# A hybrid attention and S5 block on one core: w_out split through PSUM, a second buffer for the GLU's inputs, other figures for the scheduler

## The chip, the core and the metric

The kernel runs on one core of a Trainium2 chip. Its engines are TensorE (PE, with its weight loads shown apart as PEld), VectorE (DVE), ScalarE (ACT) and GpSimd (POOL); SyncE (SP) issues nearly all DMAs. The time is device microseconds of one execution. Each engine works through its own queue in order, and an instruction that waits holds up all that stand behind it on that engine.

## What is computed

The layer normalises its input, projects it once, and feeds two groups of heads: latent attention, and an S5 state-space layer with a GELU and a GLU behind it. Each branch is gated and normalised, and both go through one output projection. Sequence 2048 + 16 meta tokens, width 1024, 8 heads (64 + 32 wide keys, 64 wide values), 32 groups of 16 channels.

```python
q = einsum('blr,re->ble', rmsnorm(q_lat, q_norm_w), w_q_up)      # + rotary part
kv = einsum('blr,re->ble', rmsnorm(kv_lat, kv_norm_w), w_kv_up)  # k_nope, v
y_attn = block_attention(qf, kf, vf)                             # softmax(q k / sqrt(96)) v
y_attn = rmsnorm(y_attn * silu(attn_gate), attn_out_norm_w)
y_ssm = gelu(s5(u, forward) + s5(u, backward) + ssm_d * u)
glu = einsum('ble,ef->blf', y_ssm, w_glu) + b_glu
y_ssm = rmsnorm(glu[..., :512] * sigmoid(glu[..., 512:]) * silu(ssm_gate), ssm_out_norm_w)
y = einsum('ble,ed->bld', concatenate([y_attn, y_ssm], -1), w_out)
return h + rmsnorm(y, post_norm_w)
```

All products of weights are made in three passes: each operand is split into a rounded high half and the low rest (`split`: ACT writes the high half, DVE subtracts it from the source for the low half), and high x high, high x low and low x high are summed in PSUM.

## The kernel before

Stages. First come projections and up-projections; then the gates' products (`pg`) run beside the S5 scan (`ssm_*`), whose last products are `py`. Behind the last `py`, `b_open` opens the pools of attention and issues the loads for it. Attention (`b_main`, `b_pv`) goes through 16 units, one for four query blocks of a pair of heads. A unit has 17 key tiles t and two heads h; for each, three products into a bank `sc`, an exponential by ACT into a buffer `pp`, an add by POOL into `acc[h]` (for the softmax's sums) and, in five groups, the products with V (`pv`). Beside unit u, `b_prep_q` makes unit u + 1's queries and their row maxima: 40 products `pm`, each followed by a `reduce_max` of DVE into `mx`; `b_kbuild` makes keys (`pk`), and `b_gate` prepares the gate `gt`. `finish` sums `acc` over partitions on PE (`sm`), takes reciprocals on DVE, sends them through DRAM (`rs_d`) to spread them over partitions (`sms`), multiplies `ot` twice on POOL and stores it to `ya_d`.

Also beside attention runs `glu_main`: it splits `w_glu` (`rawl` into `wl`), and for each of 8 blocks loads `ysv` (the S5 output) and `gv` (the gate), does GELU on DVE and ACT (`tg_c`, `ge_c`), 96 products `pa_c`, and stores `ysv` to `ys_d`. Then it loads `w_out` in eight slices (`rawo`), splits each (`wo`, the last low half is called `wo_l`) and scales the post-norm row `pw` on POOL. Only then does it start `c_stat` and `c_split`, the first steps of the output stage: `c_stat` loads a tile `yt`, squares it (`sq_c`), sums over partitions on PE (`pss`), and sends the sums through DRAM (`vvc`) to get the norm `rrc`; `c_split` splits `yt` into `yy`. `c_late` has the output products `po`, which `rrc` scales on their way out of PSUM, and `c_post` the post-norm.

What sets the order. The streams are Python generators. `Order.run` always continues the one whose inputs, banks and engine are free first by a cost model (`Clock`), and by rank among those that are free; a stream with a `due` above the current progress (in units of attention) goes after the others. `clock.lat` is what the model adds to each DMA. PE, ACT, DVE and POOL take their instructions in the order in which the streams were continued. PSUM banks go round in small rings: `pm` (banks 2, 3 and 6) is shared by row maxima, `tg`, `sm` and `pk`; the GLU has one bank. `PPB` is the number of `pp` buffers.

## Time and profile before

| | us |
|---|---|
| three timed runs | 1719.89, 1722.88, 1726.23 |
| median | 1722.88 |
| the profiled execution | 1720.63 |
| its span, first to last instruction | 1718.8 |
| PE busy in the span | 1654.9 (96%) |
| DVE, POOL, ACT busy | 1111.9 (65%), 819.4 (48%), 771.0 (45%) |
| mean granted clock of PE | 0.982 |

In the rows, L190 is a helper through which every instruction passes, so instructions are told apart by their tiles. A row of the timeline has the start and the length in us, the engine, the instruction with its output and inputs, their shapes, how many in a row were merged, and, in brackets, how long the engine stood before it and what ended that. PE's share says little by itself: what counts is where PE stands, and at what clock it goes on after that.

### The profile page before, as it was taken

The numbers are of one execution on the slowest core, as the hardware profiler recorded it, in microseconds if no ns is written. First come the engines' busy times: TensorE is split into PE (matmuls) and PEld (weight loads), VectorE is DVE, ScalarE is ACT, GpSimd is POOL, SyncE is SP. The second block draws the span as 40 slices with busy tenths as digits, with TensorE's granted clock in tenths as the row PEclk, the third lists the DMA queues.
The fourth block names the chain that finished last, engine by engine and source line by source line (L and its number), as shares of the span: only waits on it lengthen the run. The fifth ranks groups of instructions, "written<-read, shape, count | busy, mean of one in ns | idle before, by whom it ended". The sixth has DMA issues, their size and how long they took to land.

```text
span 1718.8 us, 28550 instructions
## 1 busy us (share of the span) xinstructions
PE 1654.9 (96%) x10320; PEld 1287.8 (75%) x10320; DVE 1111.9 (65%) x2531; ACT 771.0 (45%) x1604; POOL 819.4 (48%) x690
## 2 busy tenths in 40 slices
PE   7999999999999999999999999999998989989998
PEld 7897999999899866767757666776665655557776
DVE  5788635899994657555555647556555676476665
ACT  4543334445453255445444544445354534534442
POOL 0011012000000177776767688687788877862222
PEclk9999999999999999999999999999999999999999
DMA  8865735554354642012112110202012111124332
GB/s 214 269 202 142 224 125 169 145 174 145 102 164 129 171 117 82 22 54 75 38 53 72 50 58 29 90 26 70 29 40 71 41 56 43 38 99 141 119 114 86
DMA packets 179539, 175.68 MB, mean 102 GB/s; under 512 B 35419, under 2 KB 153110, under 8 KB 178118
## 3 DMA queue, kind: packets, MB, share of 16 engines
q1 hardware_dynamic: 179382, 173.86, 33.2%
q8 instruction: 81, 1.33, 0.3%
q14 instruction: 60, 0.49, 0.1%
q10 hardware_dynamic: 16, 0.00, 0.0%
HBM read 110.28 MB, written 63.54 MB: 101 GB/s over the span
## 4 chain that ended last, share of the span: by engine, by line
PE 69%; DVE 16%; DMA 6%; issue 4%; ACT 2%; SPq 1%; POOL 0%; DVEq 0%; ACTq 0%; POOLq 0%
PE sc L190 21%; PE po L190 9%; PE pm L190 8%; PE pa_c L190 5%; PE pg L190 4%; PE pu L190 3%; PE pa L190 3%; DVE w L190 2%; DVE wo L190 1%; DVE mct L190 1%; DVE s0t L190 1%; DVE r L190 1%; DMA sms<-rs_d 1%; PE pq L190 1%; DVE xx L190 1%
## 5 line engine op out<-in xcount | busy, mean ns | idle before, releaser
L190 POOL TENSOR_TENSOR acc<-acc,pp 128x512 f32<-128x512 f32 (+1 forms) x480 | 606.3, 1294 | 97.3 <-ACT pp L190 95.6
L190 ACT ACTIVATE pp<-sc 128x512 f32<-128x512 f32 (+1 forms) x544 | 320.3, 597 | 342.2 <-PE sc L190 308.7
L190 DVE TENSOR_REDUCE mx<-pm 128x1 f32<-128x412 f32 (+1 forms) x640 | 339.7, 578 | 144.5 <-PE pm L190 142.0
L190 PE MATMUL sc<-qh,kh 97*128 97x512 f32 (+1 forms) x544 | 224.4, 413 | 2.4 <-DVE qh L190 2.4
L190 PE MATMUL sc<-qh,kl 96*128 96x512 f32 (+1 forms) x544 | 220.7, 406 | 0.0
L190 PE MATMUL sc<-ql,kh 96*128 96x512 f32 (+1 forms) x544 | 218.5, 402 | 0.0
L190 PE MATMUL pm<-kh,qh 96*128 96x412 f32 (+1 forms) x640 | 196.1, 369 | 20.1 <-DVE mx L190 17.5
L190 PE MATMUL po<-wo,yy 128*128 128x512 f32 (+1 forms) x759 | 180.8, 391 | 0.0
L190 PEld LDWEIGHTS pm<-kh,qh 96*128 96x128 f32 x640 | 119.1, 194 | 78.9 <-DVE mx L190 27.6
L190 PEld LDWEIGHTS po<-wo,yy 128*128 128x128 f32 x759 | 139.7, 189 | 35.2 <-issue 3.0
L190 PE MATMUL pg<-x2h,wg_h 128*128 128x256 f32 x448 | 131.2, 293 | 3.8 <-ACT gs L190 3.8
L190 PEld LDWEIGHTS sc<-qh,kh 97*128 97x128 f32 (+1 forms) x544 | 102.3, 188 | 38.1 <-issue 19.2
L190 PE MATMUL pg<-x2h,wg_l 128*128 128x256 f32 x448 | 127.9, 286 | 0.0
L190 PE MATMUL pg<-x2l,wg_h 128*128 128x256 f32 x448 | 127.8, 285 | 0.0
L190 PEld LDWEIGHTS sc<-ql,kh 96*128 96x128 f32 (+1 forms) x544 | 103.1, 189 | 28.1
L190 POOL TENSOR_TENSOR ta<-qs,cs 128x512 f32<-128x512 f32 x8 | 10.9, 1363 | 222.0 <-ACT qs L190 148.4
L190 PEld LDWEIGHTS sc<-qh,kl 96*128 96x128 f32 (+1 forms) x544 | 103.3, 190 | 11.0
L190 POOL TENSOR_TENSOR t_c<-o_c,pw 128x512 f32<-128x512 f32 (+1 forms) x33 | 44.9, 1362 | 135.1 <-DVE o_c L190 118.9
L190 POOL COPY U<-um 128x4 f32<-128x4 f32 x16 | 4.8, 309 | 209.1 <-issue 145.2
L190 PE MATMUL pa_c<-gh,wl 128*128 128x256 f32 x512 | 103.8, 284 | 0.0
L190 PEld LDWEIGHTS pg<-x2h,wg_h 128*128 128x128 f32 x448 | 87.0, 194 | 4.8 <-ACT gs L190 4.4
L190 PEld LDWEIGHTS pa_c<-gh,wl 128*128 128x128 f32 x512 | 84.0, 190 | 6.7 <-issue 2.4
(456 smaller groups left out, 3364.7 us busy)
## 6 DMA issues: line engine op xcount, KB each, us to landing
raw<-in_x_dram SPq DMA_DIRECT2D x16, 512.0 KB
gate_d<-gs SPq DMA_DIRECT2D x64, 128.0 KB
md<-g_d SPq DMA_DIRECT2D x64, 128.0 KB
xt_c<-in_x_dram SPq DMA_DIRECT2D x8, 1024.0 KB
out_dram<-o_c SPq DMA_DIRECT2D x15, 512.0 KB
xt_d<-x3h SPq DMA_DIRECT2D x14, 512.0 KB
xt_d<-x3l SPq DMA_DIRECT2D x14, 512.0 KB
x2h<-xt_d SPq DMA_DIRECT2D x14, 512.0 KB
```

What stands on the lines that cost most here:

```text
L190: r = f(*args, **kw)
```

## The change

- `w_out`: each slice is now split in two halves of 512 columns. ACT writes the scaled half into a PSUM bank of the ring `pm` (`ws_o`), ACT copies it to the high half, and DVE subtracts with `ws_o` from PSUM as an input. Before, ACT scaled the whole slice into the high half, and DVE did scale and subtraction in one instruction with all inputs in SBUF. The due times go from 12.1 + 0.35 k to 12.6 + 0.36 k (+ 0.18 for the second half).
- `rawl` and `ysv`, which share a tag, have two buffers instead of one; the blocks' due times are 1.42 units apart instead of 1.3, and the products within a block are packed into 1.2 instead of 1.3.
- `clock.lat` is 4.0 instead of 2.0 from `b_open` on, and 2.2 instead of 0.95 after each unit.
- In unit 15 the sums of the last two key tiles go to DVE instead of POOL (four adds).
- `PPB` is 12 instead of 13, and `ones` has 32 columns instead of 64.
- In `ssm_x` the scheduler may turn to other streams between the four groups of scaled copies.

```diff
@@ -299,7 +299,7 @@
     cp = Pool(clock, "cp", ctx.enter_context(tc.tile_pool(name="cp", bufs=1, side="left")), 0.0)
     ident = cp.tile([P, P], F32, name="ident")
     make_identity(nc, ident)
-    ones = cp.tile([P, 64], F32, name="ones")
+    ones = cp.tile([P, 32], F32, name="ones")
     POOL.memset(ones, 1.0)
     cols = cp.tile([P, 27], F32, name="cols")
     half = cp.tile([P, 1], F32, name="half")
@@ -1387,6 +1387,7 @@
                 A.copy(xx[64:128, ri, 1, :, ::-1], xq[64:128])
 
             for o, x_, k in ((w1, xr, 0), (w2, xr, 1), (vr, vi, 2), (xr, vi, 0)):
+                yield Need(eng="A")
                 for q in range(NB):
                     c = slice(q * P, (q + 1) * P)
                     A.activation(o[:, c], x_[:, c], AF.Copy, scale=l8[:, k, b * NB + q:b * NB + q + 1])
@@ -1440,7 +1441,7 @@
     kh, kl, vps, qts = {}, {}, {}, {}
 
     def b_open():
-        clock.lat = 2.0
+        clock.lat = 4.0
         kp = open_pool("kp", "left")
         qp = open_pool("qp", "left")
         kw = open_pool("kw", "left")
@@ -1570,7 +1571,7 @@
             done[f"q{u}"] = 1
 
     FR = -1.5
-    PPB = 13
+    PPB = 12
     pps, accs = {}, {}
 
     gts = {}
@@ -1647,13 +1648,13 @@
                     if t == 1:
                         POOL.tensor_tensor(acc[h], first[h], pp, ALU.add)
                     elif t > 1:
-                        POOL.tensor_tensor(acc[h][:n], acc[h][:n], pp[:n], ALU.add)
+                        (V if u == 15 and t >= NJ - 1 else POOL).tensor_tensor(acc[h][:n], acc[h][:n], pp[:n], ALU.add)
                     if t == 0:
                         first.append(pp)
                     pps.setdefault((u, t), []).append(pp)
                     order.progress = u + (t + 0.5 * h + 0.5) / 17
             done["unit"] = u + 1
-            clock.lat = 0.95
+            clock.lat = 2.2
 
     def b_pv():
 
@@ -1687,7 +1688,7 @@
         NT = 256
         wl = gl.tile([P, 2, 4, D], F32R, name="wl")
         for k in range(4):
-            raw = gl.tile([P, D], F32, tag="ysv", name="rawl", bufs=1)
+            raw = gl.tile([P, D], F32, tag="ysv", name="rawl", bufs=2)
             SP.dma_start(raw, w_glu[k * P:(k + 1) * P, :].rearrange("(g h) f -> h g f", h=16))
             yield Need(raw, when=lambda: order.progress > 0.05)
             for hv in range(2):
@@ -1698,7 +1699,7 @@
                 split(wl[:, 0, k, c], wl[:, 1, k, c], ws)
         for b in range(8):
             bs = slice(b * NT, (b + 1) * NT)
-            ysv = gl.tile([P, 4, NT], F32, tag="ysv", name="ysv", bufs=1)
+            ysv = gl.tile([P, 4, NT], F32, tag="ysv", name="ysv", bufs=2)
             for t in range(2):
                 SP.dma_start(ysv[:, :, t * P:(t + 1) * P],
                              yr_d[:, 2 * b + t].rearrange("m h (g c) -> (h g) m c", c=P))
@@ -1706,7 +1707,7 @@
             SP.dma_start(gv, gate_d[4:8, :, bs].rearrange("m p c -> p m c"))
             gh = gl.tile([P, 4, NT], F32R, tag="gh", name="gh", bufs=1)
             gl_ = gl.tile([P, 4, NT], F32R, tag="sq", name="gl_", bufs=1)
-            d0 = 0.5 + b * 1.3
+            d0 = 0.5 + b * 1.42
 
             for hv in range(2):
                 h_ = slice(2 * hv, 2 * hv + 2)
@@ -1733,7 +1734,7 @@
                     for k in range(4):
                         if k % 2 == 0:
                             yield Need(gl_, banks=["gl"] if (half_, k) == (0, 0) else [],
-                                       due=d0 + (mm_ + 1) * 1.3 / 18)
+                                       due=d0 + (mm_ + 1) * 1.2 / 18)
                             mm_ += 1
                             if (half_, k) == (0, 0):
                                 pa = pst("gl", "pa_c")
@@ -1762,8 +1763,12 @@
 
                 yield Need(when=lambda: "q15" in done)
                 st["wo"][1].append(pools["qp"].tile([P, D], F32R, tag="q4", name="wo_l7", bufs=1))
-            yield Need(raw, eng="A V", due=12.1 + k * 0.35)
-            split(st["wo"][0][k], st["wo"][1][k], raw, cols[:, AOW + k:AOW + k + 1])
+            for hv in range(2):
+                c = slice(hv * 512, hv * 512 + 512)
+                yield Need(raw, eng="A V", banks=["pm"], due=12.6 + k * 0.36 + hv * 0.18)
+                ws = pst("pm", "ws_o")
+                A.activation(ws, raw[:, c], AF.Copy, scale=cols[:, AOW + k:AOW + k + 1])
+                split(st["wo"][0][k][:, c], st["wo"][1][k][:, c], ws)
         yield Need(st["pw"], eng="P")
         POOL.tensor_scalar(st["pw"], st["pw"], -0.5, None, ALU.mult)
         done["pw"] = 1
```

The first place is SP's queue in unit 1 and 2, where the inputs of the GLU's second and third block are loaded (`ysv`, `gv`). Before:

```order
L190 DMA gt<-gate_d 128x512
L190 DMA rs_d<-sms 4x256
L190 DMA sms<-rs_d 128x1x512
L190 DMA ya_d<-ot 128x512
L190 DMA gv<-gate_d 128x4x256
L190 DMA ys_d<-ysv 128x4x256
L190 DMA ysv<-yr_d 128x4x128 x2
L190 DMA kv<-kvt_d 128x2x412 x2
```

After:

```order
L190 DMA ya_d<-ot 128x512
L190 DMA ysv<-yr_d 128x4x128 x2
L190 DMA kv<-kvt_d 128x2x412
L190 DMA q_9607<-qn_d 64x2x512
L190 DMA q_9607<-qr_d 16x2x512 x2
L190 DMA gt<-gate_d 128x512
L190 DMA rs_d<-sms 4x256
L190 DMA sms<-rs_d 128x1x512
L190 DMA gv<-gate_d 128x4x256
L190 DMA ys_d<-ysv 128x4x256
L190 DMA ya_d<-ot 128x512
L190 DMA ysv<-yr_d 128x4x128 x2
```

The load of `ysv` for the second block moved ahead of the store of the first (`ys_d<-ysv`), and `gv` ahead of `ya_d<-ot`; the last row is the third block's load.

The second place is DVE in units 13 and 14, from the row maxima's end (`nm`) of one unit on; `qh` are the maxima put into the queries. Before:

```order
L190 TENSOR_REDUCE nm<-mx 128x8
L190 SCALAR_TENSOR_TENSOR wo<-rawo,cols,wo 128x1024
L190 CAST qh_14704<-pt_m 1x128 x4
L190 CAST qh_14708<-pt_m 1x128 x4
L190 TENSOR_REDUCE mx<-pm 128x1 x2
L190 RECIPROCAL sms<-sms 128x64 x2
L190 TENSOR_REDUCE mx<-pm 128x1 x2
L190 RECIPROCAL sms<-sms 128x64
L190 TENSOR_REDUCE mx<-pm 128x1
L190 RECIPROCAL sms<-sms 128x64
L190 TENSOR_REDUCE mx<-pm 128x1 x4
L190 SCALAR_TENSOR_TENSOR wo<-rawo,cols,wo 128x1024
```

After:

```order
L190 TENSOR_REDUCE nm<-mx 128x8
L190 TENSOR_TENSOR wo<-ws_o,wo 128x512
L190 CAST qh_14715<-pt_m 1x128 x4
L190 CAST qh_14719<-pt_m 1x128 x4
L190 TENSOR_TENSOR wo<-ws_o,wo 128x512
L190 RECIPROCAL sms<-sms 128x64 x4
L190 TENSOR_REDUCE mx<-pm 128x1 x21
L190 SCALAR_TENSOR_TENSOR gt<-tg,gt 128x512
L190 TENSOR_REDUCE mx<-pm 128x1 x13
L190 TENSOR_TENSOR wo<-ws_o,wo 128x512
L190 TENSOR_REDUCE mx<-pm 128x1 x2
L190 TENSOR_TENSOR wo<-ws_o,wo 128x512
```

The steps on `w_out` moved out of the first row maxima of a unit to its last ones and behind them, and the reciprocals stand together ahead of the maxima.

The third place is the end of attention. PE, from the last products with V (`pv`) on, before:

```order
L190 MATMUL pv__16078<-pp,vp 64x512 x8
L190 MATMUL po_16380<-wo,yy 128x512 x12
L190 MATMUL po_16381<-wo,yy 128x512 x6
L190 MATMUL sm<-acc_16032,ones 32x256 x2
L190 MATMUL sm<-acc_16033,ones 32x256 x2
L190 MATMUL po_16381<-wo,yy 128x512 x4
```

After:

```order
L190 MATMUL pv__16105<-pp,vp 64x512 x8
L190 MATMUL sm<-acc_16067,ones 32x256 x2
L190 MATMUL sm<-acc_16068,ones 32x256 x2
L190 MATMUL pss<-sq_c,ones 32x128 x4
L190 MATMUL po_16445<-wo,yy 128x512 x12
```

DVE at the same place, from the last step on `w_out` on, before:

```order
L190 SCALAR_TENSOR_TENSOR wo_l_15981<-rawo,cols,wo 128x1024
L190 TENSOR_TENSOR sq_c<-sq_c 128x512
L190 TENSOR_TENSOR sq_c<-sq_c 128x256
L190 RECIPROCAL sms<-sms 128x64 x3
L190 TENSOR_TENSOR yy<-yt,yy 128x1024
L190 RECIPROCAL sms<-sms 128x64
L190 TENSOR_TENSOR sq_c<-sq_c 128x512
L190 TENSOR_TENSOR sq_c<-sq_c 128x256
L190 TENSOR_TENSOR yy<-yt,yy 128x1024
L190 COPY sq_c<-pss 128x128
```

After:

```order
L190 SCALAR_TENSOR_TENSOR gt<-tg,gt 128x512
L190 TENSOR_TENSOR acc_16067<-acc_16067,pp 128x512
L190 TENSOR_TENSOR acc_16068<-acc_16068,pp 128x512
L190 TENSOR_TENSOR acc_16067<-acc_16067,pp 16x512
L190 TENSOR_TENSOR acc_16068<-acc_16068,pp 16x512
L190 RECIPROCAL sms<-sms 128x64 x4
L190 TENSOR_TENSOR yy<-yt,yy 128x1024 x2
L190 TENSOR_TENSOR sq_c<-sq_c 128x512
L190 TENSOR_TENSOR sq_c<-sq_c 128x256
L190 TENSOR_TENSOR sq_c<-sq_c 128x512
L190 TENSOR_TENSOR sq_c<-sq_c 128x256
L190 COPY sq_c<-pss 128x128
```

The output products ahead of `sm` are gone; `yy` and `sq_c`, which stood ahead of unit 15's reciprocals, stand behind them, and `pss` behind `sm`.

## Rows read from the trace of the kernel before

**Rows 1.** Stretches: length; busy us of PE, PEld, DVE, ACT, POOL; PEclk; DMA; GB/s

```profile
320.00:480.00 160.00, 155.64 (x1809) 150.44 (x1810) 155.43 (x346) 80.99 (x220) 2.87 (x20) 1.00 0.46 138
...
718.70:793.00 74.30, 71.44 (x376) 51.37 (x378) 38.93 (x78) 30.52 (x58) 45.18 (x36) 0.95 0.18 56
...
851.70:916.30 64.60, 60.58 (x301) 41.54 (x303) 34.90 (x70) 28.46 (x52) 44.97 (x36) 0.95 0.22 65
1262.90:1311.50 48.60, 48.60 (x224) 30.45 (x226) 26.05 (x54) 22.68 (x39) 45.15 (x37) 1.00 0.13 47
1311.50:1367.50 56.00, 51.41 (x226) 32.38 (x224) 36.53 (x57) 25.00 (x42) 47.62 (x38) 0.94 0.18 59
1367.50:1423.40 55.90, 51.37 (x224) 31.68 (x223) 38.23 (x57) 25.11 (x42) 45.92 (x37) 0.97 0.15 50
1423.40:1479.50 56.10, 51.96 (x226) 32.87 (x228) 36.35 (x57) 24.33 (x40) 45.78 (x36) 0.94 0.10 33
```

**Rows 2.** Timeline in unit 12: start, length, instruction, count [pause before]

```profile
1319.78 7.16 DVE L190 SCALAR_TENSOR_TENSOR wo<-rawo,cols,wo 128x1024 fp32r<-128x1024 f32 x1 [0.95 <-ACT wo L190]
...
1320.93 4.92 POOL L190 TENSOR_TENSOR acc<-acc,pp 128x512 f32<-128x512 f32 x4
...
1327.49 1.70 PE L190 MATMUL pm<-kh,qh 96*128 96x412 f32 x3 [4.59 <-DVE mx L190]
```

**Rows 3.** The same view as rows 1, of the stretch behind that pause

```profile
1326.30:1333.10 6.80, 5.61 (x14) 4.47 (x15) 4.82 (x10) 1.19 (x2) 2.68 (x3) 0.50 0.36 134
```

**Rows 4.** Forms on the tiles wo and ws: ns min/median/max, first and last start

```profile
L190 DVE SCALAR_TENSOR_TENSOR wo<-rawo,cols,wo x7: 1442/4572/7156, 1319.8 to 1431.7; 128x1024 fp32r<-128x1024 f32 x7
...
L190 ACT ACTIVATE ws<-rawl,half x8: 668/686/693, 616.3 to 666.7; 128x512 f32<-128x512 f32 x8
L190 ACT CAST wl<-ws x8: 585/585/587, 617.0 to 667.4; 128x512 fp32r<-128x512 f32 x8
L190 DVE TENSOR_TENSOR wl<-ws,wl x8: 691/692/693, 617.6 to 668.1; 128x512 fp32r<-128x512 f32 x8
```

**Rows 5.** Timeline of ACT in unit 2 and of PE in unit 4

```profile
744.93 0.60 ACT L190 ACTIVATE ge_c<-ysv 128x512 f32<-128x512 f32 x1 [5.19 <-DMA ysv<-yr_d]
...
877.54 1.21 PE L190 MATMUL pm<-kh,qh 96*128 96x412 f32 x2 [4.02 <-DVE mx L190]
```

**Rows 6.** The chain of waits in unit 1: start, us, what

```profile
706.21 2.87 PE pa_c L190 x24
```

**Rows 7.** Timeline of DVE ahead of the first score

```profile
585.67 17.35 DVE L190 TENSOR_REDUCE mx<-pm 128x1 f32<-128x412 f32 x32
```

**Rows 8.** Timeline at the end of attention: PE, POOL, ACT, DVE

```profile
1517.21 4.47 PE L190 MATMUL po<-wo,yy 128*128 128x512 f32 x18
1525.84 1.07 PE L190 MATMUL sm<-acc,ones 128*32 128x256 f32 x4 [4.16 <-POOL acc L190]
1527.06 1.07 PE L190 MATMUL sm<-acc,ones 128*32 128x256 f32 x4 [0.15 <-POOL acc L190]
...
1471.55 2.77 POOL L190 TENSOR_SCALAR pw<-pw 128x1024 f32<-128x1024 f32 x1
...
1542.84 1.49 POOL L190 TENSOR_TENSOR ot<-ot,sms 128x512 f32<-128x512 f32 x1 [3.54 <-DMA sms<-rs_d]
...
1528.17 0.37 ACT L190 COPY sms<-sm 128x256 f32<-128x256 f32 x1 [2.79 <-PE sm L190]
...
1536.73 1.05 ACT L190 CAST yy<-yt 128x1024 fp32r<-128x1024 f32 x1 [0.99 <-PE po L190]
...
1531.75 1.78 DVE L190 RECIPROCAL sms<-sms 128x64 f32<-128x64 f32 x4
1533.44 1.08 DVE L190 TENSOR_TENSOR sq_c<-sq_c 128x512 f32<-128x512 f32 x2
...
1539.51 1.21 DVE L190 TENSOR_TENSOR yy<-yt,yy 128x1024 fp32r<-128x1024 f32 x1
...
1550.81 0.74 DVE L190 SCALAR_TENSOR_TENSOR o_c<-po,rrc,o_c 128x512 f32<-128x512 f32 x1
```

## The prediction, made before the changed kernel ran

> **What bounds the kernel now.** I cut the span into stretches first: granted clock and busy time of each engine, one stretch for each attention unit (from the `sm` products of one unit to those of the next). TensorE (PE) is busy nearly throughout, so a gain can only come from its pauses and from the clock behind them. Unit 11 (1262.9 to 1311.5) has nothing but the common work of a unit: 102 score products, 40 row-max products, 34 pairs with V. It takes 48.6 us, PE busy all of it at clock 1.00 [rows 1]. Units 12, 13 and 14 hold the same products and take 56.0, 55.9 and 56.1 at clock 0.94 to 0.97 [rows 1]: 7.4 + 7.3 + 7.5 = **22.2 us** over unit 11. Units 2 and 4 are long as well, but GLU products lie in them; I take those off below.
>
> Then the timeline at one pause. In unit 12 the VectorE (DVE) instruction that makes the low half of a slice of `w_out` starts at 1319.78 and lasts 7.16 us. GpSimd (POOL) runs adds back to back until 1325.85, and DVE ends 1.1 us after that [rows 2]. The row maxima are queued behind it on DVE, their PSUM banks stay full, and PE stands 4.59 us before a `pm` product [rows 2]. In the next 6.8 us the granted clock is 0.50, the 1.2 GHz level; unit 11 runs at 2.4 GHz throughout [rows 1, 3]. The seven such DVE instructions of one name take 1.44 to 7.16 us, though they have one shape [rows 4]: the time goes by what POOL does. 4.6 us of pause and half of the slow stretch are what unit 12 lacks.
>
> The GLU's pauses are of another kind. At 744.93 ScalarE (ACT) has waited 5.19 us for the transfer of `ysv`; GELU steps of DVE wait for ACT, and row maxima stand behind them. The same pattern in unit 4 ends a pause of PE of 4.02 us at 877.54 [rows 5].
>
> **The change part by part.**
>
> *w_out by way of PSUM.* Eight DVE instructions, most of them long, become sixteen `tensor_tensor` with one input in PSUM. The trace has that very form: the split of `w_glu`, 0.69 us in all eight cases [rows 4], in a stretch in which POOL was adding. ACT has 0.69 + 0.585 for each half [rows 4], 16 x 1.27 = 20 us even if nothing of its old work went, over three units in which it is busy 25 of 56 [rows 1]: hidden by its idle time. New is that each half takes a turn on the three banks of the row maxima and holds it for 0.69 + 0.585 + 0.69 = 2.0 us. PE has two other banks meanwhile. I take the whole 22.2 us as gained; ends: 22.2, and 11 if half of the pauses come back as waits for a bank.
>
> *Second buffer for `rawl` and `ysv`, later due times of the GLU.* By SP's rows the load of a block's `ysv` stands one block ahead: it no longer waits for the store of the block before. `gv` still has one buffer, but stands ahead of `ya_d<-ot` on SP now, so not behind POOL. Gain: a GLU product costs 0.12 us (24 in 2.87) [rows 6]. Unit 2 has 144 of them and 6 products for K (at 0.2): 74.3 - 48.6 - 17.3 - 1.2 = 7.2. Unit 4 has 72 and 3: 64.6 - 48.6 - 8.6 - 0.6 = 6.8 [rows 1]. Together **14.0 us**. What is late next in these units is `gv`; in most blocks about ten row maxima lie between the old block's end and its use on DVE. Ends: 14 and 7.
>
> *Scheduler's clock (4.0 and 2.2 for 2.0 and 0.95).* It costs no instruction; it orders consumers of transfers later. Between the last `py` and the first score the K build now stands behind 18 more gate products, which takes away PE's waits for `kv`. But the first score waits for DVE's row maxima, of which 32 run back to back for 17.35 us at the end [rows 7]. In the new order fewer are left after the last K product, which itself comes 2 to 3 us later: 0, with ends of 2 either way.
>
> *Yield in the S5 scan's ACT steps.* Copies of gate tiles slip between the scaled copies, and PE's waits for them go. But DVE is busy 155.4 of 160 us there [rows 1]: PE only runs out of filler sooner. 0; ends -2 and +2.
>
> *PPB 12.* An exponential waits for the add 12 tiles back, not 13. POOL is busy 45 of 48.6 us in a full unit [rows 1], so it keeps up and this is hidden; if it lagged everywhere, one add of 1.23 us in 16 units, 20 us. Of `ones` only 32 columns are read by products: nothing.
>
> *The end of attention.* This is where the order costs. The scheduler places the `pw` step by POOL's clock. The last `w_out` step now falls into unit 15, where POOL has a backlog, so `pw` lands behind all its adds, and the streams `c_stat` and `c_split`, which start after it, with it. Before, squares and splits of the first two output tiles were done in unit 15, and 18 output products from 1517.21 covered part of the wait for `sm` (1525.84, after a pause of 4.16); both `sm` groups were done at 1528.1 [rows 8]. Without that cover these output products would have begun at 1528.1 - 18 x 0.24 = 1523.8. Now no product stands between the last `pv` and `sm`; and behind `sm` PE's queue has `pss`, which DVE feeds only after the reciprocals, two `yy` and four `sq_c` instructions. From `sm` on: products 0.6, copy 0.37, then on ACT square and cast 1.05 + 1.05 (the reciprocals, 1.78, lie beside them), DVE `yy` 2 x 1.21 and `sq_c` 2 x 1.08, `pss` 0.35: **8.0 us** [rows 8], during which PE has nothing.
>
> When is `sm`? PE's last `pv` ends at about 1517 as before. Four adds leave POOL (4 x 1.23 = 4.9) and go to DVE (0.6 each, by `yy`, which has twice the columns): from POOL's old end, 1527, this gives 1527 - 4.9 + 2.4 = 1524.5. Better: POOL's product with `sms`, which waited for a transfer in unit 15, now stands four adds later. Worse: POOL goes straight on to `pw`, 2.77 us [rows 8], and both inputs of the four sums lie in SBUF, as in the instruction that POOL held up for four adds [rows 2]: 1527.2 if they wait for it. Ends 1518 and 1527.2; I take 1521, so 1521 + 8.0 - 1523.8 = 5.2 lost. The Trainium skill (SBUF — State Buffer, Who interferes with whom) says that a DVE instruction with two SBUF inputs and a GpSimd one that reads SBUF exclude each other for the length of one instruction. By it DVE would be in after one add, ahead of `pw` (rival 5); the row of unit 12, where it was kept out over four, does not agree.
>
> On top, the third segment of output products needs the norm of tile 0. It stands on SP behind `ya_d<-ot`: reciprocals at `sm` + 2.8, return trip 9.3 (1533.5 to 1542.8), product 1.5, from there 6.5 to the first use of `rrc` [rows 8]: `sm` + 20.1, while PE is there at 8.0 + 48 x 0.24 = 19.5; 0.6, and 0.7 for freeing the bank. Lost in all: **7 us**, ends 4 and 14.
>
> **Sum.** Against the profiled execution: 1718.8 - 22.2 - 14.0 + 7 + 1 (small new waits) = 1690.6; that run was 1.8 longer than its span: 1692.4. It lies 2.3 below the median of the three shown; I put the prediction at **1693**.
>
> **Rivals.**
> 1. *The end costs nothing* (`sm` at 1518, part of the chain before `pss` beside it): 1693 - 7 = 1686. For it: POOL may no longer wait in that unit. Against: the rows behind `sm` are a serial chain.
> 2. *Half of the `w_out` pauses come back*, as waits for a bank or for ACT, whose copies stand behind exponentials: 1693 + 11 = 1704.
> 3. *The change doesn't do what it says*: DVE's long time isn't POOL's doing, and the halves are held up as well: 1693 + 22 = 1715. Against it: eight times 0.69.
> 4. *Slower*: each half stops PE for the 2.0 us that it holds a row-max bank. 16 x 2.0 = 32, and one slow stretch a unit (half of 6.8), 3 x 3.4 = 10: 1693 + 42 = 1735. It decides from 30 / 16 = 1.9 us of PE time a half on. Against it: there are three banks.
> 5. *DVE's sums get in between two POOL instructions*: `sm` at 1519 and `pw` beside them, 2 us sooner than I took: 1691. It is the rule of the page named above.
>
> **How the numbers follow.** Forecast 0.57 (1693), rival 1 0.12, rival 2 0.11, rival 5 0.10, rival 3 0.05, rival 4 0.05. A measurement of this kernel tells about 0.5% from no change, 8.6 us, so under 1714.3 is faster: forecast and rivals 1, 2 and 5, 0.90; rival 3 is within, rival 4 slower. Range 1684 to 1708: down to rival 1 with the 2 of the S5 stretch, up to rival 2 with 4 of the end's upper bound; rivals 3 and 4 and the tails are left out.
>
> **What would show it.** DVE `wo` at 0.7 us each and units 12 to 14 at 48 to 50 us, clock 1.00: the first term. No pause of PE over 1 us in the units with GLU products: the second. A pause of some 8 us between `sm` and `pss`, with the slow clock behind it: the third. The forecast is wrong if ACT's `ws_o` stands late behind exponentials and PE waits for `pm` banks in units 12 to 14, or if the first score comes over 3 us later than the new start of the K build explains.

## The result

The changed kernel takes **1695.8 us** (median of four runs, 1692.8 to 1698.1), the kernel before 1721.5 beside it: ratio 0.9845, interval 0.9818 to 0.9872. The profiled execution took 1692.8, its span is 1691.0 us (before: 1718.8), PE is busy 1641.0 us of it at a mean granted clock of 0.990.

Where the 27.8 us of span went, cut at the starts of the `sm` products and at the end of the last `pv`:

| stretch | before | after | difference | predicted |
|---|---|---|---|---|
| start to unit 0's `sm` | 657.2 | 656.0 | -1.2 | 0 |
| units 1 to 11 | 654.3 | 639.2 | -15.1 | -14.0 |
| units 12 to 14 | 168.0 | 145.9 | -22.1 | -22.2 |
| unit 15 to the last `pv`'s end | 37.8 | 38.1 | +0.3 | 0 |
| last `pv`'s end to the end | 201.6 | 211.9 | +10.3 | +7 |

(One more us had been set aside for small waits.) The same stretches as in [rows 1], now of the changed kernel: 320 to 480, units 2 and 4, units 12, 13 and 14, and the slow stretch at the end of attention. Columns are length, busy us of PE, PEld, DVE, ACT, POOL with instructions, granted clock, DMA share, GB/s.

```profile
320.00:480.00 160.00, 158.99 (x1836) 153.82 (x1835) 153.89 (x341) 77.06 (x209) 3.76 (x20) 1.00 0.46 137
716.98:777.20 60.22, 60.22 (x319) 42.13 (x317) 34.34 (x70) 27.63 (x51) 45.04 (x36) 1.00 0.15 47
837.31:891.49 54.18, 54.18 (x270) 36.33 (x268) 31.25 (x62) 25.84 (x47) 42.50 (x34) 1.00 0.25 77
1295.15:1343.80 48.65, 48.65 (x223) 30.54 (x221) 28.39 (x57) 25.03 (x45) 44.81 (x36) 1.00 0.15 47
1343.80:1392.42 48.62, 48.62 (x223) 30.53 (x221) 30.14 (x60) 29.05 (x51) 44.89 (x36) 1.00 0.18 58
1392.42:1441.03 48.61, 48.61 (x223) 30.53 (x221) 29.45 (x59) 27.49 (x49) 44.84 (x36) 1.00 0.18 60
1483.41:1497.06 13.65, 6.59 (x22) 4.04 (x23) 6.58 (x11) 4.27 (x5) 0.30 (x1) 0.50 0.44 131
```

In units 2, 4 and 12 to 14 PE is busy for the whole length at clock 1.00. Units 12 to 14 are as long as unit 11 was [rows 1]; the clock no longer falls between 610 and 1483 us. The steps on `w_out`, by form (minimum, median, maximum in ns), answer [rows 4]:

```profile
L190 ACT ACTIVATE ws_o<-rawo,cols x16: 670/688/720, 1321.9 to 1447.6; 128x512 f32<-128x512 f32 x16
L190 ACT CAST wo<-ws_o x16: 587/587/589, 1322.7 to 1448.4; 128x512 fp32r<-128x512 f32 x16
L190 DVE TENSOR_TENSOR wo<-ws_o,wo x14: 681/692/693, 1323.3 to 1435.1; 128x512 fp32r<-128x512 f32 x14
```

DVE takes 0.68 to 0.69 us for each half, where the seven whole slices took 1.44 to 7.16. The end of attention, by the timeline of PE, DVE, POOL and ACT, answers [rows 8]:

```profile
1475.37 3.80 PE L190 MATMUL pv__16105<-pp,vp 128*64 128x512 f32 x16
1482.78 1.67 PE L190 MATMUL sm<-acc,ones 128*32 128x256 f32 x8 [3.61 <-DVE acc L190]
1490.27 0.64 PE L190 MATMUL pss<-sq_c,ones 128*32 128x128 f32 x4 [5.82 <-DVE sq_c L190]
1492.15 0.64 PE L190 MATMUL pss<-sq_c,ones 128*32 128x128 f32 x4 [1.24 <-DVE sq_c L190]
...
1477.02 6.31 DVE L190 TENSOR_TENSOR acc<-acc,pp 128x512 f32<-128x512 f32 x4 [16.83 <-POOL acc L190]
...
1486.80 2.36 DVE L190 TENSOR_TENSOR yy<-yt,yy 128x1024 fp32r<-128x1024 f32 x2
1489.08 1.15 DVE L190 TENSOR_TENSOR sq_c<-sq_c 128x512 f32<-128x512 f32 x2
1490.94 1.15 DVE L190 TENSOR_TENSOR sq_c<-sq_c 128x512 f32<-128x512 f32 x2 [0.72 <-ACT sq_c L190]
...
1459.56 18.66 POOL L190 TENSOR_TENSOR acc<-acc,pp 128x512 f32<-128x512 f32 x15
1478.16 2.80 POOL L190 TENSOR_SCALAR pw<-pw 128x1024 f32<-128x1024 f32 x1
...
1484.77 1.06 ACT L190 ACTIVATE sq_c<-yt 128x1024 f32<-128x1024 f32 x1
1485.73 1.98 ACT L190 CAST yy<-yt 128x1024 fp32r<-128x1024 f32 x2
1489.85 1.06 ACT L190 ACTIVATE sq_c<-yt 128x1024 f32<-128x1024 f32 x1 [2.15 <-DVE sq_c L190]
```

PE's last `pv` ends at 1479.2. It waits 3.61 us for DVE's sums before `sm`, then 5.82 and 1.24 before the two halves of `pss`; the first output product starts at 1492.72. POOL goes from add to add from 1459.56 on, and the first of DVE's four sums, issued at 1477.02, is done only at 1479.77: the four sums take 6.31 us, the first 2.75 and the third 2.44, the other two 0.68 and 0.67.

The S5 scan has a pause that the kernel before lacks: PE stands 4.68 us for a copy of ACT.

```profile
492.89 3.08 PE L190 MATMUL z<-U,mbt 128*64 128x128 f32 x30 [4.68 <-ACT mbt L190]
```

### The profile page after: what moved, and what is told of

It is laid out like the page before. It is cut to its first block, busy times and chain, and to the rows that moved or that the text cites. A ratio compares the mean times of both kernels' runs of the same rounds, so it can differ in the third digit from the quotient of the medians.

```text
span 1691.0 us, 28589 instructions
## 1 busy us (share of the span) xinstructions
PE 1641.0 (97%) x10320; PEld 1278.0 (76%) x10320; DVE 1082.2 (64%) x2543; ACT 781.4 (46%) x1628; POOL 805.8 (48%) x686
## 5 line engine op out<-in xcount | busy, mean ns | idle before, releaser
L190 POOL TENSOR_TENSOR acc<-acc,pp 128x512 f32<-128x512 f32 (+1 forms) x476 | 595.2, 1283 | 87.4 <-ACT pp L190 86.9
L190 PE MATMUL sc<-qh,kh 97*128 97x512 f32 (+1 forms) x544 | 220.7, 406 | 1.8 <-DVE qh L190 1.8
L190 PE MATMUL sc<-qh,kl 96*128 96x512 f32 (+1 forms) x544 | 217.0, 399 | 0.0
L190 PE MATMUL pm<-kh,qh 96*128 96x412 f32 (+1 forms) x640 | 187.9, 359 | 0.6 <-ACT qh L190 0.2
L190 PEld LDWEIGHTS sc<-qh,kl 96*128 96x128 f32 (+1 forms) x544 | 101.1, 186 | 10.8
```

The source lines that it names most:

```text
L190: r = f(*args, **kw)
```

## Experiments

Runs whose names begin with b_ are edits of the kernel before, those with a_ of the changed kernel. A unit's length is given less its GLU products (0.12 us each, [rows 6]). Each ratio is to the kernel before on the same chip. The first 320 us, in which no edit changes the order, differ by up to 5.6 us between profiled executions, so effects are read from stretches further on. Where a run is set beside the changed kernel's 1695.8, the kernel before took 1719.7 to 1721.5 beside them, so a difference of two or three us is not told from none.

### w_out alone, by way of PSUM

```diff
-            yield Need(raw, eng="A V", due=12.1 + k * 0.35)
-            split(st["wo"][0][k], st["wo"][1][k], raw, cols[:, AOW + k:AOW + k + 1])
+            for hv in range(2):
+                c = slice(hv * 512, hv * 512 + 512)
+                yield Need(raw, eng="A V", banks=["pm"], due=12.1 + k * 0.35 + hv * 0.175)
+                ws = pst("pm", "ws_o")
+                A.activation(ws, raw[:, c], AF.Copy, scale=cols[:, AOW + k:AOW + k + 1])
+                split(st["wo"][0][k][:, c], st["wo"][1][k][:, c], ws)
```

> The kernel before with one edit: w_out in halves of 512 columns by way of PSUM, as in the change, but with the due times of before (12.1 + 0.35 k, + 0.175 for the second half). Buffers, the scheduler's clock, the sums of unit 15 and the end of attention are those of before: the 18 output products still stand ahead of the last sm. Theory (DVE is kept out by POOL while its inputs lie in SBUF, and not while one lies in PSUM): the 16 DVE steps take 0.69 us each, units 12 to 14 take 48.6 us each instead of 56, the pauses of 4.6 us ahead of pm and the slow stretches behind them are gone, the GLU's pauses in units 2 and 4 stay: 22 us less than before, about 1699. Rival A (each half holds a bank of the row maxima, half of the pauses return): about 1710. Rival B (the gain of the change came from its later due times, not from PSUM): DVE is late as before, about 1721.

Measured: 1702.9 us, ratio 0.990 (0.9884 to 0.9916), 18.0 us less. Units 12 to 14 take 48.6, 48.6 and 48.7: the theory's 22 us are there, and rivals A and B fall. Four us went elsewhere. In unit 15 (timeline of DVE, POOL and PE):

```profile
1460.39 12.08 DVE L190 TENSOR_TENSOR yy<-yt,yy 128x1024 fp32r<-128x1024 f32 x1
...
1458.86 7.65 POOL L190 TENSOR_TENSOR acc<-acc,pp 128x512 f32<-128x512 f32 x6
1466.47 1.25 POOL L190 TENSOR_TENSOR ot<-ot,gt 128x512 f32<-128x512 f32 x1
1467.69 3.69 POOL L190 TENSOR_TENSOR acc<-acc,pp 128x512 f32<-128x512 f32 x3
...
1473.99 0.64 PE L190 MATMUL pss<-sq_c,ones 128*32 128x128 f32 x4 [7.75 <-DVE sq_c L190]
```

DVE's `yy`, both inputs in SBUF, starts at 1460.39 and ends at 1472.47; POOL goes from instruction to instruction, nine of them from then on, until 1471.38. A step of 1.2 us took 12.08, the sums for `pss` stand behind it, and PE waits 7.75 us. In the kernel before, the same step in the same order took 1.81 us, also beside a POOL that went from add to add; there the adds took longer (six in 10.30):

```profile
1482.92 1.81 DVE L190 TENSOR_TENSOR yy<-yt,yy 128x1024 fp32r<-128x1024 f32 x1 [0.39 <-ACT yy L190]
...
1480.92 10.30 POOL L190 TENSOR_TENSOR acc<-acc,pp 128x512 f32<-128x512 f32 x6
```

The mechanism was removed from `w_out` and caught another instruction. (In return the pause ahead of the last `sm` went: POOL caught up meanwhile.)

### w_out in halves, but from SBUF

```diff
-            yield Need(raw, eng="A V", due=12.1 + k * 0.35)
-            split(st["wo"][0][k], st["wo"][1][k], raw, cols[:, AOW + k:AOW + k + 1])
+            for hv in range(2):
+                c = slice(hv * 512, hv * 512 + 512)
+                yield Need(raw, eng="A V", due=12.1 + k * 0.35 + hv * 0.175)
+                split(st["wo"][0][k][:, c], st["wo"][1][k][:, c], raw[:, c], cols[:, AOW + k:AOW + k + 1])
```

> The kernel before with each slice of w_out split in two halves of 512 columns with the due times of the run b_wout_psum, but straight from SBUF as before: DVE reads the raw half and the high half, both in SBUF. It tells the source in PSUM from the shorter instruction. Theory (POOL keeps DVE out for the whole run of back-to-back adds): several of the 16 DVE steps still take 3 to 7 us, pauses of 4 us and slow stretches stay in units 12 to 14, and the time is within 8 us of before (1713 to 1724); it may even be worse, since there are twice as many steps to be caught. Rival A (the length of the DVE instruction decides): 0.65 to 0.75 us each and 22 us less, about 1699. Rival B: the Trainium skill (SBUF - State Buffer, Who interferes with whom) has one engine kept out for one instruction of the other; by the adds' 1.23 to 1.3 us no step would then take more than about 2 us, the pauses would shrink to under 1 us, and the time would be about 1700.

Measured: 1719.9, ratio 1.0001 (0.9984 to 1.0018). Units 12 to 14 take 58.0, 56.3 and 58.0. The forms on `wo`:

```profile
L190 DVE SCALAR_TENSOR_TENSOR wo<-rawo,cols,wo x14: 779/1434/7905, 1320.3 to 1448.1; 128x512 fp32r<-128x512 f32 x14
```

Half the length, the same hold-up (up to 7.9 us). So it is the source in PSUM that frees DVE; rivals A and B fall. (The two splits also use different DVE instructions, `scalar_tensor_tensor` and `tensor_tensor`. That is not it: `yy` above, kept out for 12.08 us, is a `tensor_tensor` with both inputs in SBUF.)

### Second buffers, PPB and due times in the kernel before

```diff
-    ones = cp.tile([P, 64], F32, name="ones")
+    ones = cp.tile([P, 32], F32, name="ones")
...
-    PPB = 13
+    PPB = 12
...
-            raw = gl.tile([P, D], F32, tag="ysv", name="rawl", bufs=1)
+            raw = gl.tile([P, D], F32, tag="ysv", name="rawl", bufs=2)
-            ysv = gl.tile([P, 4, NT], F32, tag="ysv", name="ysv", bufs=1)
+            ysv = gl.tile([P, 4, NT], F32, tag="ysv", name="ysv", bufs=2)
```

> The kernel before with two buffers for rawl and ysv, and what makes room for them (PPB 12, ones with 32 columns); due times, the scheduler's clock and w_out as before. Theory (ACT's 5 us wait for ysv comes from the single buffer, whose load stands behind the store of the block before): the pauses of PE over 1 us in units 2 and 4 go, and the slow stretches of 6.8 us behind them, 14 us less than before: about 1707. Rival A (the later due times and the longer transfers on the scheduler's clock did it; the load is late by itself, or gv is late in its place): pauses of 3 to 5 us stay, 0 to 7 us less, 1714 to 1721. Rival B (one exponential buffer less lets ACT wait for POOL in every unit): units without GLU products and without steps on w_out grow from 48.7 us to 49.5 or more, 10 to 20 us lost, 1717 to 1727.

Measured: 1731.7, ratio 1.0054 (1.0029 to 1.0078): **slower**, by 10.8 us. Units 2 and 4 did shrink (57.0 to 49.2, 55.9 to 50.7), but unit 1 grew from 55.7 to 61.2, unit 8 from 49.3 to 54.5, and units 12 and 13 from 56 to 64.0 and 61.6. Unit 11, which has neither GLU products nor `w_out`, stayed at 48.6, so it isn't rival B. The next run takes PPB alone.

```diff
-    PPB = 13
+    PPB = 12
```

> The kernel before with 12 exponential buffers in place of 13, nothing else. Theory of the prediction (hidden: POOL keeps up): units without steps on w_out stay as they are (48.7 in unit 11), the time is within 2 us of before, 1718 to 1723. Rival A (an exponential waits for the add 12 tiles back in every unit): units grow by 0.8 us or more, 10 to 20 us slower. Rival B (it shifts only the order, and with it where the steps on w_out fall in POOL's runs; it is what made single steps 10.3 us long in the run b_glu_buf): units 1 to 11 as before, units 12 and 13 at 60 to 64 us, 8 to 15 us slower: 1728 to 1736.

Measured: 1729.2, ratio 1.0048 (1.0031 to 1.0065), 8.3 us slower. Unit 11 is 48.6 as before, so waits of exponentials for a buffer cost nothing there (ACT does wait for an add now and then, in this run as in the kernel before, for up to 3.9 and 4.5 us). Unit 1 is 61.0, unit 8 54.1, units 12 and 13 62.2 each, and unit 2 is 50.0, unit 4 50.6 with a single `ysv` buffer. In units 12 and 13 that is rival B: one buffer fewer changes the order, and with it where a step falls in POOL's run. Units 1 and 8 it had left as before; there PE stands 3.98 us for `qh` and 2.90 for `gt` of DVE. And with a single `ysv` buffer ACT's waits for the transfer of `ysv`, 5.19, 5.82 and 1.88 us in the kernel before, are gone too: the change of order alone takes them away. In unit 12:

```profile
1333.40 10.56 DVE L190 SCALAR_TENSOR_TENSOR wo<-rawo,cols,wo 128x1024 fp32r<-128x1024 f32 x1 [0.74 <-ACT wo L190]
...
1328.06 14.81 POOL L190 TENSOR_TENSOR acc<-acc,pp 128x512 f32<-128x512 f32 x12
...
1344.51 1.21 PE L190 MATMUL pm<-kh,qh 96*128 96x412 f32 x2 [8.62 <-DVE mx L190]
```

When DVE's step was issued eight adds had still to end, where it had been the four of [rows 2] and one under way: 10.56 us, and PE stands 8.62. The second buffers add nothing that can be measured to this (1731.7 against 1729.2). Then the GLU's due times on top of them:

```diff
-            d0 = 0.5 + b * 1.3
+            d0 = 0.5 + b * 1.42
-                                       due=d0 + (mm_ + 1) * 1.3 / 18)
+                                       due=d0 + (mm_ + 1) * 1.2 / 18)
```

> The run b_glu_buf with the changed kernel's due times for the GLU as well (1.42 units apart, 1.2 for the products within a block); the scheduler's clock and w_out stay as before. There, units 2 and 4 lost their pauses, but unit 1 grew by 5.5 us, unit 8 by 5.2, and from unit 0's sm to unit 11's it took 652.5 us against 654.3 before and 639.2 in the changed kernel. Theory A (the later due times are what the buffers need): 639 to 643 us for these units. Theory B (the scheduler's clock is what is needed; unit 1's loss is the K build behind late transfers): 648 us or more, with a pause ahead of pk in unit 1. Units 12 to 14 hold w_out straight from SBUF and cost 56 us or more each under either; the time is within 10 us of before.

Measured: 1722.2, ratio 1.0018 (0.9999 to 1.0036), 9.6 us under b_glu_buf. Units 1 to 11 take 645.6 us, 6.9 less than in b_glu_buf: between the two theories. Unit 8 is back at 49.2; unit 1 stays at 60.9, with a pause of 2.18 us ahead of `pk`.

### The scheduler's clock

```diff
-        clock.lat = 4.0
+        clock.lat = 2.0
-            clock.lat = 2.2
+            clock.lat = 0.95
```

> The changed kernel with the scheduler's clock of before (2.0 and 0.95 for 4.0 and 2.2). Theory of the prediction (it only orders consumers of transfers later, 0 with ends of 2 either way): within 2 us of the changed kernel's 1695.8, ratio 0.984 to 0.986 to before. Rival (the longer transfers are what lets the second buffers pay: without them consumers are queued ahead of their data, as in unit 1 of the run b_glu_buf): unit 1 takes 61 us less its GLU products instead of 55.3, one or two other units 3 to 5 us more, 6 to 12 us slower than the changed kernel.

Measured: 1704.3, ratio 0.9907 (0.9876 to 0.9938), 8.5 us slower than the changed kernel. The rival holds for the time and for unit 1; no other unit up to 11 is more than 0.8 us longer. Unit 1 takes 60.8 in place of 55.3, and PE stands ahead of products for K whose input is still under way:

```profile
569.50 0.80 PE L190 MATMUL pk<-kv,wk 128*128 128x412 f32 x3 [2.66 <-DMA kv<-kvt_d]
...
669.68 1.37 PE L190 MATMUL pk<-kv,wk 128*128 128x412 f32 x3 [2.49 <-DMA kv<-kvt_d]
```

In the changed kernel PE has no wait of over 1.1 us ahead of a `pk`. Only the second of these pauses lies in unit 1; a pause like the first, ahead of the first `pk`, comes with the changed clock as well (2.09 us in the run a_half).

### The yield in the S5 scan

```diff
             for o, x_, k in ((w1, xr, 0), (w2, xr, 1), (vr, vi, 2), (xr, vi, 0)):
-                yield Need(eng="A")
```

> The changed kernel without its yield between the four groups of scaled copies in the S5 scan. In the changed kernel's trace PE waits there 4.7 us for the copy of mbt at 492.89, with 3.4 us at clock 0.5 behind it, the only pause over 2 us ahead of the end of attention; before, there was none of that kind, but many of about 0.5 to 1.4 us for gs copies. Theory (the prediction's: DVE bounds the scan, PE only runs out of other work sooner; 0, with ends of 2 either way): the pause goes, the short waits come back, the first score stands within 2 us of 604.4, and the time is within 2 us of the changed kernel's (ratio to before 0.983 to 0.987). Rival (the new pause costs what it is long): 4.8 + 1.7 = 6 us faster than the changed kernel, ratio 0.981. Rival on the other side (the short waits that the yield took away were worth more): 3 to 5 us slower, ratio 0.987 or more.

Measured: 1697.5, ratio 0.9867 (0.9851 to 0.9883): no difference from the changed kernel that can be told. The pause at 492.9 is gone, the waits of 1.1 to 1.4 us for copies are back, the first score comes at 599.9 in place of 604.4, and units 1 and 2 take 5.8 us more (59.2 and 50.6, against 55.3 and 48.7). The first rival (0.981) falls; the second (0.987 or more) is not told from the theory by the time. The theory missed the first score, which it had within 2 us. So the yield is not idle: it costs some us ahead of the first score and gives them back in units 1 and 2. (Five runs with one and the same order up to there have the first score between 601.7 and 609.9; the two without the yield at 599.9 and 603.9, 285.3 and 285.5 us after the scan's first product, the five 286.6 to 292.5.)

Set beside the two runs above, this shows that the clock and the yield only work together in units 1 to 11 (the four kernels differ otherwise only in what comes behind these):

| | units 1 to 11, us |
|---|---|
| clock and yield as before (b_glu_buf_due) | 645.6 |
| the yield alone (a_lat_old) | 645.4 |
| the clock alone (a_no_yield) | 645.0 |
| both (the changed kernel) | 639.2 |

In the first three, unit 1 has 96 GLU products, a pause of PE of 2.1 to 2.5 us and a granted clock of 0.95; with both it has 48, no pause of over 0.6 us and clock 1.00.

### w_out from SBUF again, in the changed kernel

```diff
-            for hv in range(2):
...
+            yield Need(raw, eng="A V", due=12.6 + k * 0.36)
+            split(st["wo"][0][k], st["wo"][1][k], raw, cols[:, AOW + k:AOW + k + 1])
```

> The changed kernel with the split of w_out put back to whole slices straight from SBUF, with the changed due times (12.6 + 0.36 k); everything else as changed. Theory (the parts add up): 22 us slower than the changed kernel, about 1718, DVE steps up to 7.2 us. Rival (how long POOL keeps DVE out goes by the run of adds in which the step falls, and the other edits lengthened these runs: in the runs b_glu_buf and b_glu_buf_due single steps took 10.3 to 10.9 us and units 12 and 13 62 to 64 us): two or three units of 60 us and more, 28 to 40 us slower than the changed kernel, 1724 to 1736, no better than the kernel before. Second rival (the later due times bring the steps into POOL's gaps): under 12 us slower, under 1708.

Measured: 1717.4, ratio 0.9977 (0.996 to 0.9993), 21.6 us slower than the changed kernel: the theory's 22, though one step is longer than its 7.2. Units 12 to 14 take 55.5, 57.3 and 53.2.

```profile
L190 DVE SCALAR_TENSOR_TENSOR wo<-rawo,cols,wo x7: 1283/1670/9389, 1324.6 to 1445.6; 128x1024 fp32r<-128x1024 f32 x7
```

Three steps were caught, for 8.2, 9.4 and 7.2 us, the other five were not (1.3 to 2.0).

### The end of attention

First the four sums back on POOL:

```diff
-                        (V if u == 15 and t >= NJ - 1 else POOL).tensor_tensor(acc[h][:n], acc[h][:n], pp[:n], ALU.add)
+                        POOL.tensor_tensor(acc[h][:n], acc[h][:n], pp[:n], ALU.add)
```

> The changed kernel with the last four sums of unit 15 back on POOL. In the changed kernel they took DVE 6.31 us, since POOL's adds kept the first out for 2.1 us and its product with gt the third for 1.8 us; sm came 3.6 us after the last pv. Theory (by those rows): POOL's adds end four times 1.24 = 5.0 us later, at about 1483.1 in place of 1478.2, sm comes within 1 us of the changed kernel's 1482.8, and behind it stands the same chain to pss: the time is within 2 us of the changed kernel's, ratio to before 0.983 to 0.987. Rival (the prediction's term: DVE's sums bring sm forward by 2.5 us or more): 2.5 to 5 us slower than the changed kernel, sm 6 us or more after the last pv.

Measured: 1692.8, ratio 0.9836 (0.980 to 0.9872): no difference that can be told. `sm` comes 2.7 us after the last `pv` (changed kernel: 3.6). Moving them to DVE brought nothing that can be told: from the last `pv` to the first output product it is 13.6 us, in the changed kernel 13.5. Then the output stage's first steps ahead of `pw`:

```diff
+        order.add(c_stat(), -1)
+        order.add(c_split(), -1)
         yield Need(st["pw"], eng="P")
         POOL.tensor_scalar(st["pw"], st["pw"], -0.5, None, ALU.mult)
         done["pw"] = 1
-        order.add(c_stat(), -1)
-        order.add(c_split(), -1)
```

> The changed kernel with c_stat and c_split started ahead of the step that scales pw, nothing else. Squares, sums and splits of the first tile, and its pss, move into unit 15; behind the last sm stand only output products, and 6 of them ahead of it. Theory 1 (the loss at the end is the chain behind sm, as the prediction has it): the 6.5 us pause and half of the 13.65 us slow stretch go, output products begin 10 to 12 us sooner (about 1482 in place of 1492.7), the time is 10 to 15 us under the changed kernel's: 1682 to 1687. Rival (from the run b_wout_psum: there DVE's yy took 12.08 us in unit 15, until a run of POOL's adds ended, and PE stood 8.02 us ahead of pss): in the changed kernel POOL runs from 1447.16 to 1482 without a gap, so DVE's first sq_c or yy lands behind it, pss, which stands in PE's queue in the middle of unit 15, holds up the scores behind it for 8 to 20 us, and the time is 1690 to 1710, no better than the changed kernel.

Measured: 1683.7, ratio 0.9783 (0.9758 to 0.9809), 12.1 us under the changed kernel. Theory 1 and the rival were both right in part. From the last `pv` to the end it takes 191.1 in place of 211.9 us; but unit 15 up to the last `pv` takes 48.9 in place of 38.1, for the rival's reason, only by way of ACT and not of `pss`:

```profile
1455.12 8.71 DVE L190 TENSOR_TENSOR sq_c<-sq_c 128x512 f32<-128x512 f32 x2 [5.91 <-ACT sq_c L190]
...
1446.70 11.21 POOL L190 TENSOR_TENSOR acc<-acc,pp 128x512 f32<-128x512 f32 x9
1457.85 1.30 POOL L190 TENSOR_TENSOR ot<-ot,sms 128x512 f32<-128x512 f32 x1
1459.10 3.72 POOL L190 TENSOR_TENSOR acc<-acc,pp 128x512 f32<-128x512 f32 x3
...
1463.40 1.06 ACT L190 ACTIVATE sq_c<-yt 128x1024 f32<-128x1024 f32 x1 [7.83 <-DVE sq_c L190]
...
1466.89 0.79 PE L190 MATMUL sc<-qh,kh 97*128 97x512 f32 x1 [7.01 <-ACT pp L190]
```

DVE's first sum `sq_c` is kept out until POOL's run ends at 1462.8 (8.71 us for two that take 1.15 in the changed kernel); ACT's next square, which writes the same buffer, waits 7.83 for it, the exponentials stand behind that, and PE waits 7.01 ahead of a score.

The last edit takes away what POOL is busy with:

```diff
-                        (V if u == 15 and t >= NJ - 1 else POOL).tensor_tensor(acc[h][:n], acc[h][:n], pp[:n], ALU.add)
+                        (V if u == 15 and h == 1 else POOL).tensor_tensor(acc[h][:n], acc[h][:n], pp[:n], ALU.add)
```

> The changed kernel with one condition altered: in unit 15 DVE takes all sums of the second head (17 key tiles) instead of the last four adds of both heads. POOL then has about 24 us of work in a unit of 41, so it waits for exponentials and has gaps. By the order pss stands behind unit 15's last group of products with V but one, and 60 output products follow sm at once. Theory (DVE is kept out only while POOL goes from one instruction to the next without a wait): DVE's adds, sq_c and yy take 0.5 to 2 us each, sm starts within 2 us of the last pv, output products within 3 us of it instead of 13.5; 10 to 17 us under the changed kernel: 1679 to 1686. Rival A (POOL keeps DVE out even so, for several adds at a time): some of DVE's 17 adds take 4 us and more, sm comes 5 us or more after the last pv, the gain is under 5 us. Rival B (DVE's adds keep POOL or the output stage's first steps late): pss stops PE in unit 15 for 5 us or more, no gain.

Measured: **1678.7**, ratio 0.9758 (0.973 to 0.9785), 17.1 us under the changed kernel and 5.0 under a_stat_first. Timeline of DVE, POOL and PE in unit 15:

```profile
1463.39 3.56 DVE L190 TENSOR_TENSOR yy<-yt,yy 128x1024 fp32r<-128x1024 f32 x2 [0.91 <-ACT yy L190]
1466.87 3.46 DVE L190 TENSOR_TENSOR acc<-acc,pp 128x512 f32<-128x512 f32 x2
...
1471.94 2.24 DVE L190 TENSOR_TENSOR sq_c<-sq_c 128x512 f32<-128x512 f32 x2
...
1465.83 7.35 POOL L190 TENSOR_TENSOR acc<-acc,pp 128x512 f32<-128x512 f32 x4
1475.50 4.63 POOL L190 TENSOR_TENSOR acc<-acc,pp 128x512 f32<-128x512 f32 x3 [2.33 <-ACT pp L190]
1484.39 2.97 POOL L190 TENSOR_TENSOR acc<-acc,pp 128x512 f32<-128x512 f32 x2 [4.25 <-ACT pp L190]
...
1485.58 3.80 PE L190 MATMUL pv__16105<-pp,vp 128*64 128x512 f32 x16
1489.31 0.64 PE L190 MATMUL sm<-acc,ones 128*32 128x256 f32 x8
1489.88 5.39 PE L190 MATMUL po<-wo,yy 128*128 128x512 f32 x22
```

POOL waits for exponentials again (2.33 and 4.25 us), and DVE and POOL take turns: no DVE step of unit 15 takes over 2.31 us. Neither engine is late at the end: `sm` follows the last `pv` at once, the output products follow `sm`. From the last `pv` to the end it takes 190.9 us in place of 211.9; unit 15, in which `pss` now stands, takes 42.1 up to there in place of 38.1. (DVE gets 15 adds, not 17: the first tile needs none, and the second's stays on POOL.) Then the same without the yield:

```diff
-                        (V if u == 15 and t >= NJ - 1 else POOL).tensor_tensor(acc[h][:n], acc[h][:n], pp[:n], ALU.add)
+                        (V if u == 15 and h == 1 else POOL).tensor_tensor(acc[h][:n], acc[h][:n], pp[:n], ALU.add)
             for o, x_, k in ((w1, xr, 0), (w2, xr, 1), (vr, vi, 2), (xr, vi, 0)):
-                yield Need(eng="A")
```

> The run a_half (unit 15's sums of the second head on DVE) without the yield in the S5 scan; it is a try at a faster kernel. Theory (the two don't touch each other, and the yield is worth nothing either way): within 3 us of a_half's 1678.7, with the pause ahead of z near 492 gone, the first score 4 us sooner and units 1 and 2 together 5 to 6 us longer, as in the run a_no_yield. Rival (the pause of 4.8 to 6.0 us with its slow stretch is a cost that nothing else gives back): 5 us or more faster than a_half, under 1674.

Measured: 1680.0, ratio 0.976 (0.9726 to 0.9793), the same as a_half; the theory holds.

## Why the prediction was right, and where it was not

The forecast, 1693, and its sum hold: 1695.8 lies in the range, and the three large terms came out at 22.1, 15.1 and 10.3 for 22.2, 14.0 and 7. But the second of them came about for another reason than the one given, the third was mis-sized, and three of the terms at 0 (clock, PPB and yield) stand for parts that do change the time.

**w_out: right in size and mechanism.** The comparison of units 12 to 14 with unit 11 gave the gain to 0.1 us, and the form from the split of `w_glu` the duration (0.69). No bank wait came back (rivals 2 and 4), DVE was not held up (rival 3), and ACT's copies cost nothing. Three runs show that the input in PSUM does it: with it 0.69 us everywhere, without it up to 9.4 us, at half the length still 7.9.

**GLU: the sum right, by luck in part, the attribution wrong.** The prediction put 14 us on "second buffer, later due times", 0 on the scheduler's clock and 0 on PPB. The runs, taken one after the other, give PPB 12 alone +8.3, the second buffers +2.5 (not told from 0), the due times -9.6, the scheduler's clock -8.5. In units 1 to 11 alone the kernel before takes 654.3 (651.2 and 652.2 in the two `w_out` runs, with the same order there), PPB 12 651.8, the second buffers 652.5, the due times 645.6, and clock and yield together 639.2. So the second buffers, of which the prediction made most, show nothing that can be told: ACT's waits for `ysv` go with PPB 12 alone, and the due times give 6.9. (Whether the due times need the second buffers was not tested.) The step on the clock failed: it named what the clock takes away, PE's waits for `kv`, and then priced it by the first score alone; the price is in unit 1, 5.5 us, and needs the yield. The step on PPB failed as a statement on the part: the wait for a buffer is hidden, as it said, but the order shifts, and steps from SBUF land in longer runs of POOL. The changed kernel doesn't show that loss: in `w_out` DVE has an input in PSUM, and units 1 and 8 take 55.3 and 49.2. (That the due times and the clock are what sets the other steps anew is argued; 13 buffers in the changed kernel were not tried.) I had read the pauses off the old order and the absence of pauses off the new one, so the total stood; what each part did I could not have told from these rows.

**End of attention: right in kind, 3.3 us too small, inside its ends; rival 1 (nothing lost) falls.** Up to the first output product it cost 13.5 us from the last `pv`'s end: 3.6 to `sm` (taken: 4) and 9.9 for the chain (taken: 8.0). What the chain lacked: the `sm` products take 1.7 us in place of 0.6, since the second four wait for DVE's last sum and run at clock 0.50; and the square of the second half writes the buffer of the first, so ACT waits 2.15 us for DVE's sums before it, and DVE's second pair comes after that (0.8 more). Less the 6.5 us that the old order's own way would have taken (1517.3 to 1523.8, by the prediction's working), this is 7.0 for the 5.2 of the sum. The other 3.3 (taken: 1.3) lie behind the first output product. The 1.3 were for a wait for the norm of tile 0, and none shows: PE's only pauses of over 0.2 us there are six of 0.36 to 0.56 ahead of `pss` (2.9 us; the kernel before has three, 1.8), and 4.3 us of products run at clock 0.50. How the 3.3 divide between these is not told. The terms for the four sums were wrong one by one: POOL's 4.9 us were saved, but DVE's sums took 6.31 and not 2.4, and a_sums_pool shows the move worth nothing.

**DVE and POOL.** The sum rested on DVE being kept out over a whole run of POOL. The Trainium skill (SBUF — State Buffer, Who interferes with whom) has the lock last one instruction (rival 5). At the end of attention the first sum waited out an add and got in during `pw`: 3.6 us from `pv` to `sm`, between the two. Over nine POOL instructions (12.08 us) or eight (10.56) the traces disagree with the rule as a bound on how long DVE is kept out; in a_half, where the two take turns, they agree with it.

**S5 scan, 0: right in the sum only.** PE's short waits went, it ran out of other work sooner, and one pause of 4.68 us took their place. But the term left out what the yield does behind the scan: with the changed clock units 1 and 2 are 5.8 us shorter by it, and the later first score takes about as much. That the two cancel is luck.

## What to carry to other kernels

A DVE step with its inputs in SBUF beside a GpSimd that has a backlog can cost as much as the backlog is long (7.2 to 12.1 us here; not every such step was caught, three of eight in a_wout_undone_due): bring one input through PSUM, or give GpSimd less, so that it waits now and then. After such a fix look for the next step of the same kind; here it moved from `w_out` to the output stage's `yy` and `sq_c`, and giving DVE half of the last unit's sums was worth 17 us more. Where a scheduler sets the order, a part's price depends on the other parts. Clock and yield gave nothing in units 1 to 11 one at a time and 6 us together; one buffer fewer cost 8.3 us in the kernel before, 6.2 of them in units 12 to 14, where the changed kernel shows no loss. The total doesn't tell: the parts as measured, +8.3, +2.5, -9.6, -8.5 and -21.6, come to -28.9 beside -25.7 for the whole.

## What was new of the hardware

- How long DVE is kept out: 12.08 us for a step of 1.2 (nine POOL instructions), 10.56 (eight), 8.25 for one of 0.69 (a_stat_first), each ending 0.55 us (512 columns) or 1.1 us (1024 columns) after an instruction of POOL. In all 26 cases of over 4.4 us in the runs' traces (steps with two inputs in SBUF), POOL had then come to the end of its run and stood for 0.5 us or more; six of 4.3 us ended between two adds. It isn't always so: the same `yy` took 1.81 us in the kernel before, between adds that followed without a pause. What decides whether DVE gets in between two POOL instructions is not settled by these runs; in a_half, where POOL had about half the adds and waits of its own in unit 15, no step took over 2.31 us.
- A `tensor_scalar` of two columns with one SBUF input (`vvc`) was kept out too, for 18.3 to 18.4 us over 15 adds in the kernel before, b_wout_psum and b_wout_sbuf_halves, and for 13.6 to 14.4 in the three runs with PPB 12. There POOL did not stop: DVE came in where its adds go from 128 partitions to 16. In the kernel before:

```profile
1506.26 18.41 DVE L190 TENSOR_SCALAR vvc<-vvc 128x2 f32<-128x2 f32 x2 [9.44 <-DMA vvc<-rs_d]
...
1503.51 23.50 POOL L190 TENSOR_TENSOR acc<-acc,pp 128x512 f32<-128x512 f32 x19
```

- Steps with a source in PSUM were not held up in any of these runs: the 16 of `w_out` took 0.68 to 0.69 us in each of the eight kernels that split it so.
